# A four-layer diffusion trunk on one core: the time mixing of the even layers gathers its output channel-major, with the states as stationary operands and centred values

## The chip, the cores and the metric

The kernel runs on one core of a Trainium2 chip. The metric is the device time of one execution in microseconds (us). Engines are named as the profile does: PE is TensorE (PEld its weight loads), DVE is VectorE, ACT is ScalarE, POOL is GpSimd, SP is SyncE, which here issues DMAs.

## The reference

The reference is a trunk of four layers over 256 latent and 256 context tokens, 1024 channels, float32. Every layer has a mixer and a channel mixer, with modulation vectors from a conditioning input. In layers 0 and 2 the mixer is time mixing (RWKV-7, both directions, 8 heads of 64 channels) beside neighbourhood attention; in layers 1 and 3 it is another pair, which the change does not touch. Per head the time mixing is

```python
def step(s, inp):
    r_t, w_t, k_t, v_t, a_t, b_t = inp
    sa = jnp.einsum('bhvk,bhk->bhv', s, a_t)
    s = s * w_t[:, :, None, :] + sa[..., None] * b_t[:, :, None, :] + v_t[..., None] * k_t[:, :, None, :]
    return s, jnp.einsum('bhvk,bhk->bhv', s, r_t)
...
def readout(y, r, v, dirs, g):
    mean = jnp.mean(y, axis=-1, keepdims=True)
    var = jnp.mean(jnp.square(y - mean), axis=-1, keepdims=True)
    y = (y - mean) * lax.rsqrt(var + A_GN_EPS) * ln_g.reshape(A_HEADS, A_HEAD_DIM) + ln_b.reshape(A_HEADS, A_HEAD_DIM)
    bonus = sum(jnp.sum(r * kt * r_k, axis=-1, keepdims=True) for _, kt, _ in dirs) * v
    return ((y + bonus).reshape(g.shape) * g).astype(g.dtype)
```

The two directions' outputs are added before the readout. The state is linear in the values, row by row: each value channel has a row of the state and a channel of the output of its own. So an output less its mean over a head's channels is the output that values less their mean over these channels give.

## The kernel before

The 512 tokens stand side by side as eight chunks of 64. A unit of the time mixing is one pair of heads and one direction: 4 x 2 = 8 units in an even layer, 16 in the kernel. `pre` (L580, once per pair) reads the shifted projections, normalises the keys (key norms L598, their reciprocal root on POOL L600, the copy L567 that spreads it over channels) and transposes the values to token-major through PSUM (`transp`, L571 to L577, a copy on ACT). `front` (L610, per unit) makes decays and scaled rows, the products inside a chunk (L674, and the value product L704) and the start of a triangular inverse; `mid` (L708) merges the inverse (L888 and others) and makes for each chunk a matrix Phi that takes the state before it to the state after it, a matrix RW that takes the state to the output, G (masked products of rows inside a chunk), UV (both sources of the state) and B (what the chunk adds).

`rec` (L758) is the recurrence. It first writes the in-chunk product of all eight chunks into one PSUM bank pO (L769, 32 passes), and then walks the chunks. At each of seven steps it multiplies RW with the state and adds that into pO (the output product, L790); at six of them it also makes the next state (the state product, two passes at L784, then the decay and the addition of B on DVE, L793). Before, pO is token-major: 128 tokens by two heads of 64 channels. So that one pass serves both heads, ACT copies the two halves of a state to the diagonal blocks of a zeroed 128 x 128 tile (L789, two copies a step, four such tiles in turn):

```python
for h in range(2):
    hs = slice(64 * h, 64 * h + 64)
    nc.scalar.copy(wide[hs, hs], st[hs])
nc.tensor.matmul(pO[cs, t, :], RW[:, t, c2, :], wide, start=False, stop=d == 1, skip_group_check=True)
```

`readout` (L796, once per pair, behind its second direction) reduces pO to a mean (L802, L803), subtracts it (L806), squares (ACT, L807), reduces (L809), scales and adds the constant (L810), takes the reciprocal root on POOL (L812), scales by it (L813) and multiplies values and bonus (L816), all per token on DVE where nothing else is said. Its second half, `late` (L822), transposes result and bonus to channel-major on PE, applies the layer's scale and shift, adds, multiplies with the gate and stores.

What sets the order: the class `Pipe` (L1819) hands over, for each i, `front` of unit i, `mid` of unit i-1 in step with `rec` of unit i-2, then the `late` of the pair before, then a `readout`, all at a high priority; the large weight products of the layer (`gemm`, weights cast on ACT L190 and split on DVE L191, three passes L222 to L224) and the modulation vectors of the next layer (`mod_units`, weights mw by DMA, product L165) fill the rest. A tile scheduler takes this program, with dependences and priorities, and sets each engine's order; an engine then works its list strictly in that order.

Of the kernel before, what the change touches and what calls it, by code (L numbers as in the profile page):

```python
# [20 lines left out]
F32 = mybir.dt.float32  # L21
# [9 lines left out]
NT = 512  # L31
# [11 lines left out]
class Mixed:  # L43
    """Outputs of the mixers, channel-major, kept in DRAM by channel tile."""
# [12 lines left out]
class Net:  # L57
    def __init__(self, tc, a, ctx):
# [6 lines left out]
        # banks of PSUM by use: large products, parts of the mixers, adaLN, outputs of the mixers  # L65
# [14 lines left out]
    def load_consts(self, name, pool, tag=None, width=None):  # L80
        """A table of constants that depend on shapes alone; its parts become attributes."""
        nc = self.nc
        off, n = CONST_OFF[name]
        t = pool.tile([128, width or n], F32, name=tag or "cst_" + name)[:, :n]
        nc.sync.dma_start(t, self.a["k_" + name])
        for part, (o, w) in off.items():
            setattr(self, part, t[:, o:o + w])
# [55 lines left out]
    def mod_units(self, l, pool=None):  # L143
        """Six chunks of eight channel tiles for each stream, channel-major: [128, 48, 2].

        The weights of the first two chunks come through the pool, if one is given."""
# [9 lines left out]
        for u in range(0, 48, 8):  # L156
            if u == 16:
                pool = None
            # two units on each quarter of the partitions
# [20 lines left out]
    def unit(self, src, kt, cols):  # L180
        """src [128, kt, cols] in DRAM -> high and low tiles."""
# [12 lines left out]
    def mm3(self, out, pairs, start=True, stop=True):  # L194
        """out += sum over (lhsH, lhsL, rhsH, rhsL) of lhs.T @ rhs."""
# [7 lines left out]
    def gemm(self, W, kt, c0, cols, xh, xl, tok, done, order=None):  # L203
        """Columns c0.. of W (given as [128, kt, n]), channel-major: done(column tile, psum) for each 128."""
# [23 lines left out]
    def gemm_tok(self, W, c0, cols, xh, xl, done):  # L228
        """Columns of W, token-major: done(token tile, first column, width, psum)."""
# [21 lines left out]
    def vecs(self, pool, name, **src):  # L251
        """Vectors of multiples of 128 in DRAM, channel-major [128, n] each; they become attributes of the result."""
# [20 lines left out]
    def square_sums(self, tok):  # L273
        """Sums of h^2 over the channels, token-major: [128, token tile]."""
# [13 lines left out]
    def rstd_bcast(self, tok, ss=None):  # L288
        """1 / sqrt(mean of h^2 + eps) on all partitions: [128, tokens]."""
# [16 lines left out]
    def norm_mod(self, l, g, which, tok, ss=None):  # L306
        """nH, nL: high and low parts of the modulated RMSNorm, channel-major."""
# [124 lines left out]
def rows(x):  # L432
    """The four rows of the grid in a padded line of tokens."""
    return x[:, 1:261].rearrange("p (r w) -> p r w", w=65)[:, :, :64]


def rwkv_consts():
# [4 lines left out]
    # for a and for r, by the chunk of a tile: the mask of b on the chunk's half of the partitions, that of k on the other  # L442
# [14 lines left out]
class Rwkv:  # L457
    """Both directions of the time mixing for one layer, by pairs of heads."""
# [3 lines left out]
    def __init__(self, net, e, pool):  # L462
# [18 lines left out]
        self.sts = [pool.tile([128, 128], F32, name=f"st{i}") for i in range(4)]  # L481
        self.nst = 0
        # a of one unit, and r of three
        self.ar = pool.tile([128, 4, NT], F32, name="ar")
        self.nar = 0
        for b in [self.shb] + self.sts:
            nc.gpsimd.memset(b, 0.0)
        self.pd = {}

# [1 line left out]
    def project(self, key, i, col, nh, nl):  # L491
        """Column tile col of the input projection as tile i of a group."""
# [13 lines left out]
    def shifted(self, key, cols):  # L506
        """A group of projections, mixed with the shift of the tokens."""
# [14 lines left out]
        for i, c in enumerate(cols):  # L522
# [7 lines left out]
            else:  # L530
                # the two chunks of each tile in each other's place
# [18 lines left out]
    def tok_sums(self, prod, out):  # L550
        """out [128 tokens, tile, head] = sums over the channels of each head."""
# [4 lines left out]
    def tok_sums_swapped(self, prod, out):  # L556
        """The same, with the two chunks of each tile in each other's place."""
# [6 lines left out]
    def bcast_heads(self, small, out):  # L564
        """out [channels of two heads, tokens] from small [tokens, tile, head]."""
# [6 lines left out]
    def transp(self, src, dst):  # L572
        """dst [128, 4, 128] token-major from src [128, 512] channel-major."""
# [6 lines left out]
    def pre(self, hp):  # L580
# [9 lines left out]
        # normalised keys  # L590
# [11 lines left out]
        # token-major values, each chunk on the half of the partitions that its own rows do not use  # L602
        S["V"] = pl.tile([128, 4, 128], F32, name="V", bufs=2)
        self.transp(v, S["V"])
# [4 lines left out]
    def front(self, hp, d, S):  # L609
# [30 lines left out]
        # scaled rows: a and b (both time reversed inside chunks for d = 1), r, k  # L640
# [3 lines left out]
        # those of a chunk side by side, b first in even chunks and k in odd ones  # L644
# [16 lines left out]
        # products with a inside each chunk of a tile: those of b on the chunk's half of the partitions, those of k on the other  # L661
        Q = [n.tmp.tile([128, 4, 2, 64], F32, name=name) for name in ("nt", "sq")]
        # [rows of b and k, products with r] by chunk and head
# [18 lines left out]
        # bonus: r * k * r_k, summed over the channels of a head and over the directions  # L682
# [7 lines left out]
        # token-major copies  # L690
# [1361 lines left out]
```

## Time and profile before

| | |
|---|---|
| time, median of 3 runs (lowest to highest) | 3420.98 us (3409.43 to 3421.87) |
| span of the profiled execution | 3398.9 us |
| own time of the profiled execution | not given apart from the three runs, which are 10.5 to 23 us longer than the span |
| instructions in the profile | 63286 |
| PE / PEld busy | 92% / 71% |
| DVE / ACT / POOL busy | 56% / 38% / 15% |
| moved by DMA | 479.21 MB, mean 141 GB/s |

The profile is of one execution, by the hardware profiler. Its page gives busy time by engine; other views give the same for a stretch of time, the waits (which engine stood idle before which line, and what ended the idle time), and the instructions in order of time. A row of a wait reads "engine, tile and line that waited <- engine, tile and line (or DMA) that ended the wait". In rows of PE the start times of neighbours tell what a pass costs, since passes overlap at their ends; "64\*64" is the form of the stationary operand. A granted clock of 1.00 is TensorE's level of 2.4 GHz, and 0.50 that of 1.2 GHz.

### The profile page before, as it was taken

The page shows a single profiled execution, that of the slowest core. Times are in us where ns is not written, and L with a number is a line of the kernel's source. Part 1 is how long each engine was busy: PE and PEld are TensorE (multiplying, and loading weights), DVE is VectorE, ACT ScalarE, POOL GpSimd, SP SyncE. Part 2 cuts the span into 40 slices and gives each one's busy share as a digit, 9 for nine tenths or more (in the row PEclk, how much of TensorE's full clock was granted, in tenths as well). Part 3 has the DMA queues.
Part 4 walks back from the last instruction along what each step waited for, and adds up shares of the span by engine and source line. Part 5 has one row for each costly group of instructions (what it writes and reads, how often), then busy time and mean ns, then how long its engine had stood idle before and what let it go on. Part 6 is the DMA issues. An engine that isn't in the chain of part 4 may idle for free. (4 is left out here: it accounts for less than half of the span.)

```text
span 3398.9 us, 63286 instructions
## 1 busy us (share of the span) xinstructions
PE 3120.2 (92%) x24452; PEld 2418.1 (71%) x24452; DVE 1920.1 (56%) x4229; ACT 1291.6 (38%) x2785; POOL 515.4 (15%) x1159
## 2 busy tenths in 40 slices
PE   7999789999999889899999998877999999977998
PEld 4876456787787667578887776545787777756997
DVE  3556545766436696343434556555676445685554
ACT  3334344332235335232223333434333224534444
POOL 0223310000001653000000123220000000563000
PEclk8998889999999899899998998889999999978999
DMA  8635655345345544733336634553334334644554
GB/s 282 178 97 130 151 141 156 87 136 143 111 125 143 167 126 144 245 119 94 96 100 191 184 103 128 126 125 101 102 127 136 111 113 145 196 156 156 160 176 134
DMA packets 549696, 479.21 MB, mean 141 GB/s; under 512 B 176533, under 2 KB 480531, under 8 KB 549395
## 3 DMA queue, kind: packets, MB, share of 16 engines
q1 hardware_dynamic: 549394, 475.17, 48.5%
q8 instruction: 193, 3.16, 0.4%
q14 instruction: 109, 0.89, 0.1%
HBM read 406.34 MB, written 72.90 MB: 141 GB/s over the span
## 5 line engine op out<-in xcount | busy, mean ns | idle before, releaser
L191 DVE TENSOR_TENSOR wl<-w,wh 128x512 fp32r<-128x512 f32 x786 | 545.8, 697 | 766.4 <-ACT wh L190 746.6
L190 ACT CAST wh<-w 128x512 fp32r<-128x512 f32 x786 | 484.5, 619 | 1159.7 <-PE pb L223 343.3
L222 PE MATMUL pg<-nh,wh 128*128 128x512 f32 (+2 forms) x760 | 294.6, 388 | 19.4 <-ACT nh L270 8.7
L222 PE MATMUL pb<-nh,wh 128*128 128x512 f32 (+1 forms) x832 | 305.3, 374 | 4.0 <-ACT nh L325 2.7
L223 PE MATMUL pb<-nl,wh 128*128 128x512 f32 (+1 forms) x832 | 306.5, 371 | 0.0
L224 PE MATMUL pb<-nh,wl 128*128 128x512 f32 (+1 forms) x832 | 299.8, 373 | 0.0
L223 PE MATMUL pg<-nl,wh 128*128 128x512 f32 (+2 forms) x760 | 291.4, 383 | 0.6 <-DVE gr L1179 0.6
L224 PE MATMUL pg<-nh,wl 128*128 128x512 f32 (+2 forms) x760 | 290.4, 382 | 0.1
L298 POOL TENSOR_TENSOR nr<-nv,cst_base 128x4 f32<-128x4 f32 (+1 forms) x9 | 8.4, 938 | 1660.8 <-DVE nv L296 1660.8
L222 PE MATMUL ph<-nh,wh 128*128 128x512 f32 (+1 forms) x624 | 242.0, 388 | 10.1 <-ACT nh L325 5.9
L224 PE MATMUL ph<-nh,wl 128*128 128x512 f32 (+1 forms) x624 | 240.1, 385 | 0.0
L223 PE MATMUL ph<-nl,wh 128*128 128x512 f32 (+1 forms) x624 | 239.5, 384 | 0.0
L165 PE MATMUL px<-mw,cnd 128*32 128x256 f32 x1536 | 158.8, 450 | 83.5 <-DMA mw<-in_mod_w_dram 68.9
L222 PEld LDWEIGHTS pg<-nh,wh 128*128 128x128 f32 (+1 forms) x760 | 146.3, 193 | 56.4 <-ACT nh L270 11.3
L222 PEld LDWEIGHTS pb<-nh,wh 128*128 128x128 f32 x832 | 158.6, 192 | 36.3 <-ACT nh L325 3.2
L223 PEld LDWEIGHTS pb<-nl,wh 128*128 128x128 f32 x832 | 159.5, 192 | 29.3 <-DVE nl L271 1.3
L224 PEld LDWEIGHTS pb<-nh,wl 128*128 128x128 f32 x832 | 155.5, 191 | 30.7 <-issue 1.0
L223 PEld LDWEIGHTS pg<-nl,wh 128*128 128x128 f32 (+1 forms) x760 | 146.1, 192 | 34.8 <-issue 3.0
L224 PEld LDWEIGHTS pg<-nh,wl 128*128 128x128 f32 (+1 forms) x760 | 145.7, 192 | 29.1 <-issue 1.0
L858 POOL TENSOR_TENSOR Etmp<-E 64x14 f32<-64x14 f32 (+13 forms) x448 | 160.6, 359 | 31.1
L860 POOL TENSOR_TENSOR E<-E,Etmp 64x14 f32<-64x14 f32 (+13 forms) x448 | 158.8, 354 | 32.9
L222 PEld LDWEIGHTS ph<-nh,wh 128*128 128x128 f32 x624 | 119.6, 192 | 39.7 <-ACT nh L325 6.7
(578 smaller groups left out, 6440.8 us busy)
## 6 DMA issues: line engine op xcount, KB each, us to landing
mw<-in_mod_w_dram SPq DMA_DIRECT2D x192, 512.0 KB
w<-in_f_gate_dram SPq DMA_DIRECT2D x176, 256.0 KB
w<-in_f_up_dram SPq DMA_DIRECT2D x176, 256.0 KB
w<-in_f_down_dram SPq DMA_DIRECT2D x176, 256.0 KB
w<-in_w_in_even_dram SPq DMA_DIRECT2D x104, 256.0 KB
w<-in_w_in_odd_dram SPq DMA_DIRECT2D x80, 256.0 KB
w<-in_w_out_dram SPq DMA_DIRECT2D x64, 256.0 KB
hd<-hT SPq DMA_DIRECT2D x32, 256.0 KB
```

The source lines that it names most:

```text
L165: nc.tensor.matmul(p[32 * c:32 * c + 32, :256], self.cnd[:, k, :], wt[:, 256 * c:256 * c + 256], start=k == 0, stop=k == KT - 1, skip_grou ...
L190: nc.scalar.copy(wh[:, :n], w[:, :n])
L191: nc.vector.tensor_tensor(wl[:, :n], w[:, :n], wh[:, :n].bitcast(F32), op=ALU.subtract)
L222: nc.tensor.matmul(o, wh[:, kk, m:m + mm], xh[:, k, tok], start=i == 0, stop=False)
L223: nc.tensor.matmul(o, wh[:, kk, m:m + mm], xl[:, k, tok], start=False, stop=False)
L224: nc.tensor.matmul(o, wl[:, kk, m:m + mm], xh[:, k, tok], start=False, stop=i == kt - 1)
L298: nc.gpsimd.tensor_tensor(r, v, self.mhalf[:, :nt], op=ALU.pow)
L858: nc.gpsimd.tensor_tensor(o, E[:, :s, s:s + 1].to_broadcast([m8, s, v]), E[:, s:s + 1, s + 1:].to_broadcast([m8, s, v]), op=ALU.mult)
L860: nc.gpsimd.tensor_tensor(E[:, :s, s + 1:], E[:, :s, s + 1:], o, op=ALU.add)
```

## The change

The output bank pO becomes channel-major: two heads of 64 channels on the partitions, eight chunks of 64 tokens. For the in-chunk product the operands trade places (UV stationary, G moving), and a pass writes the partition half of its head instead of its chunk's. The output product becomes two passes of 64 x 64 per step, with the state as stationary operand and RW moving; the copies to the wide tiles and these tiles are gone, with their eight zero fills on POOL. Since a mean over a head's channels would now run over partitions, `pre` subtracts from the values their mean over each head, and keeps that mean. `readout` copies pO to SBUF (ACT), squares it (ACT), sums the squares per token with `tok_sums` (PE, eight passes into a bank of PSUM), and takes scale and root as before; values and bonus are multiplied after the mean was added back, by halves of the partitions. `late` spreads the reciprocal root over channels (`bcast_heads`: a copy on DVE, four transposes on PE) and multiplies with it on DVE, before layer scale and shift; the transposes of the result are gone. Line numbers move by some lines, since comments are left out in the changed file. The diff, without that:

```diff
 class Rwkv.__init__
-        self.sts = [pool.tile([128, 128], F32, name=f"st{i}") for i in range(4)]
-        self.nst = 0
-        for b in [self.shb] + self.sts:
-            nc.gpsimd.memset(b, 0.0)
+        nc.gpsimd.memset(self.shb, 0.0)
 pre
-        self.transp(v, S["V"])
+        pv = n.bank("f")
+        for t in range(4):
+            nc.tensor.transpose(pv[:, t * 128:(t + 1) * 128], v[:, t * 128:(t + 1) * 128], n.ident)
+        pv = pv.rearrange("p (a c) -> p a c", c=64)
+        S["mean"] = mean = pl.tile([128, 8], F32, name="mean", bufs=4)
+        nc.vector.tensor_reduce(mean, pv, axis=AX.X, op=ALU.add)
+        nc.vector.tensor_scalar(mean, mean, 1.0 / 64, None, op0=ALU.mult)
+        nc.vector.tensor_tensor(S["V"].rearrange("p t (h c) -> p (t h) c", h=2), pv,
+                                mean[:, :, None].to_broadcast([128, 8, 64]), op=ALU.subtract)
 rec
-            S["pO"] = n.bank("o", (128, 4, 128))
+            S["pO"] = n.bank("o", (128, 8, 64))
...
-                    nc.tensor.matmul(pO[64 * c2:64 * c2 + 64, t, hs], G[:, 1, 2 * t + c2, h, :], UV[:, t, c2, hs],
-                                     start=d == 0 and t == 0 and h == 0, stop=False, skip_group_check=True)
+                    nc.tensor.matmul(pO[hs, 2 * t + c2, :], UV[:, t, c2, hs], G[:, 1, 2 * t + c2, h, :],
+                                     start=d == 0 and t == 0 and c2 == 0, stop=False, skip_group_check=True)
...
-            wide = self.sts[self.nst % 4]
-            self.nst += 1
             for h in range(2):
                 hs = slice(64 * h, 64 * h + 64)
-                nc.scalar.copy(wide[hs, hs], st[hs])
-            nc.tensor.matmul(pO[cs, t, :], RW[:, t, c2, :], wide, start=False, stop=d == 1, skip_group_check=True)
+                nc.tensor.matmul(pO[hs, c, :], st[hs], RW[hs, t, c2, :], start=False, stop=d == 1, skip_group_check=True)
 readout
-        mean = n.tmp.tile([128, 8], F32, name="mean")
-        nc.vector.tensor_reduce(mean, o, axis=AX.X, op=ALU.add)
-        nc.vector.tensor_scalar(mean, mean, 1.0 / 64, None, op0=ALU.mult)
         y, sq = yt.tile(), yt.tile()
-        c = y.rearrange("p (a v) -> p a v", v=64)
-        nc.vector.tensor_tensor(c, o, b8(mean), op=ALU.subtract)
-        nc.scalar.activation(sq, y, AF.Square)
+        nc.scalar.copy(y, pO)
+        s2 = n.tmp.tile([128, NT], F32, name="sq")
+        nc.scalar.activation(s2, y, AF.Square)
+        ps = n.bank("b")
+        self.tok_sums(s2, ps)
         var = n.tmp.tile([128, 8], F32, name="var")
-        nc.vector.tensor_reduce(var, sq.rearrange("p (a v) -> p a v", v=64), axis=AX.X, op=ALU.add)
-        nc.vector.tensor_scalar(var, var, 1.0 / 64, 64e-5, op0=ALU.mult, op1=ALU.add)
+        nc.vector.tensor_scalar(var, ps[:, :8], 1.0 / 64, 64e-5, op0=ALU.mult, op1=ALU.add)
...
-        nc.vector.tensor_tensor(c, c, b8(rs), op=ALU.mult)
...
-            nc.vector.tensor_tensor(sq[p].rearrange("p (t h v) -> p t h v", t=4, h=2),
-                                    S["d"][1]["UV"][p, :, c2].rearrange("p t (h v) -> p t h v", h=2),
-                                    S["bonus"][p].rearrange("p (t h) -> p t h", h=2)[:, :, :, None].to_broadcast([64, 4, 2, 64]),
-                                    op=ALU.mult)
+            z = sq[p].rearrange("p (a v) -> p a v", v=64)
+            u = z.rearrange("p (t h) v -> p t h v", h=2)
+            nc.vector.tensor_tensor(u, S["d"][1]["UV"][p, :, c2].rearrange("p t (h v) -> p t h v", h=2),
+                                    S["mean"][p].rearrange("p (t h) -> p t h", h=2)[:, :, :, None].to_broadcast([64, 4, 2, 64]),
+                                    op=ALU.add)
+            nc.vector.tensor_tensor(z, z, b8(S["bonus"], p), op=ALU.mult)
 late
-            pt = n.bank("b")
-            for t in range(4):
-                nc.tensor.transpose(pt[:, t * 128:(t + 1) * 128], y[:, t * 128:(t + 1) * 128], n.ident)
-            nc.scalar.activation(y, pt, AF.Identity, scale=self.lg[:, hp:hp + 1], bias=self.lb[:, hp:hp + 1])
+            pr = n.bank("b")
+            self.bcast_heads(rs, pr)
+            nc.vector.tensor_tensor(y, y, pr, op=ALU.mult)
+            nc.scalar.activation(y, y, AF.Identity, scale=self.lg[:, hp:hp + 1], bias=self.lb[:, hp:hp + 1])
```

Since a scheduler sets the order, three places of it follow, before and after. On PE, the first two steps of the first recurrence (pb is a PSUM bank of parts of the mixer, po the output bank, st a state, Bst the first one, L888 the inverse and L674 the chunk products of other units); before:

```order
L784 MATMUL pb<-Bst,Phi 64x64 [waits DVE_49]
L784 MATMUL pb<-Bst,Phi 64x64
L790 MATMUL po<-st_426,RW 64x128 [waits Activation_49]
L888 MATMUL pb<-Yb,Rinv 16x16 x24
L674 MATMUL pf<-ar,bk 128x128 [waits DVE_49]
L674 MATMUL pf<-ar,bk 128x128 [waits PE_49]
L674 MATMUL pf<-ar,bk 128x128 x6
L888 MATMUL pb<-Yb,Rinv 16x16 x7
L784 MATMUL pb<-st,Phi 64x64 [waits DVE_49]
L784 MATMUL pb<-st,Phi 64x64
L790 MATMUL po<-st_427,RW 64x128 [waits Activation_49]
```

and the same place in the changed kernel, where the state product is L790, the output product L793, and the other units' lines are L889 and L680:

```order
L790 MATMUL pb<-Bst,Phi 64x64 [waits DVE_49]
L790 MATMUL pb<-Bst,Phi 64x64
L793 MATMUL po<-RW,Bst 64x64 x2
L889 MATMUL pb<-Yb,Rinv 16x16 [waits Activation_49]
L889 MATMUL pb<-Yb,Rinv 16x16 x20
L680 MATMUL pf<-ar,bk 128x128 [waits DVE_49]
L680 MATMUL pf<-ar,bk 128x128 [waits PE_49]
L680 MATMUL pf<-ar,bk 128x128 x6
L889 MATMUL pb<-Yb,Rinv 16x16 x11
L790 MATMUL pb<-st,Phi 64x64 [waits DVE_49]
L790 MATMUL pb<-st,Phi 64x64
L793 MATMUL po<-RW,st 64x64 x2
```

The output product stands behind the state product in both; what moved is that it no longer waits for ACT and comes as two passes.

On DVE, `pre` of the first pair of heads (kn are the key norms, kr POOL's reciprocal root, wl a weight's low part, lw a decay); before:

```order
L598 TENSOR_SCALAR kn<-pf 128x8 [waits PE_49]
L567 COPY nt<-kr 128x512 [waits Pool_49]
L191 TENSOR_TENSOR wl<-w,wh 128x512 [waits DVE_49,DMAHW4_49,PE_49,Activation_49]
L191 TENSOR_TENSOR wl<-w,wh 128x512 [waits DMAHW7_49,PE_49,Activation_49]
L621 TENSOR_SCALAR lw<-lw 128x512 [waits Activation_49]
```

and now:

```order
L595 TENSOR_SCALAR kn<-pf 128x8 [waits PE_49]
L607 TENSOR_REDUCE mean<-pf 128x8 [waits PE_49]
L608 TENSOR_SCALAR mean<-mean 128x8 [waits DVE_49]
L609 TENSOR_TENSOR V<-pf,mean 128x512 [waits DVE_49]
L564 COPY nt<-kr 128x512 [waits Pool_49]
L191 TENSOR_TENSOR wl<-w,wh 128x512 [waits DMAHW4_49,PE_49,Activation_49]
L191 TENSOR_TENSOR wl<-w,wh 128x512 [waits DMAHW7_49,PE_49,Activation_49]
L627 TENSOR_SCALAR lw<-lw 128x512 [waits Activation_49]
```

The three instructions on the values came in between the key norms and the copy that waits for POOL.

On ACT, around the second readout (yo is a tile of outputs, naqk and naqh are queries and keys of the attention, naP its weights); before:

```order
L732 COPY UV<-pb 64x2x128 x2
L1016 ACTIVATE naP,sm<-pg,mx 128x256 [waits DVE_49]
L1024 COPY naPT<-ph 128x4x128 [waits PE_49]
L807 ACTIVATE yo<-yo 128x512 [waits DMAHW6_49,DVE_49]
L620 ACTIVATE lw<-pf,w0h 128x512 [waits PE_49]
```

and now:

```order
L738 COPY UV<-pb 64x2x128 x2
L803 COPY yo<-po 128x512 [waits PE_49]
L998 CAST naqk<-naqk 64x512 [waits DMAHW3_49]
L805 ACTIVATE sq<-yo 128x512 [waits Activation_49]
L270 CAST naqh<-naqk 128x512 [waits DMAHW4_49]
L997 CAST nakh<-naqk 64x512
```

The square before waited for DVE's subtraction; now it follows ACT's own copy of the bank, with a cast that waits for a DMA between the two.

## Rows read from the trace of the kernel before

**Rows 1.** The page: busy time by engine, and TensorE's granted clock in 40 equal slices (tenths).

```profile
PE 3120.2 (92%) x24452; PEld 2418.1 (71%) x24452; DVE 1920.1 (56%) x4229; ACT 1291.6 (38%) x2785; POOL 515.4 (15%) x1159
...
PEclk8998889999999899899998998889999999978999
```

**Rows 2.** Stretches from:to in us; length, busy per engine, clock, DMA share, GB/s.

```profile
100.00:290.00 190.00, 183.72 (x1981) 144.84 (x1979) 107.49 (x249) 72.85 (x164) 47.81 (x135) 0.97 0.47 126
290.00:560.00 270.00, 221.35 (x2944) 139.80 (x2943) 153.98 (x385) 118.00 (x313) 62.52 (x139) 0.82 0.58 142
```

**Rows 3.** Waits of PE, 100 to 2400 us: total us, times, longest.

```profile
PE px L165 <- DMA mw<-in_mod_w_dram: 50.9, 33, 6.3
...
PE pb L784 <- DVE st L793: 6.9, 5, 3.6
```

**Rows 4.** Same stretches as rows 2, L790 alone: PE, PEld, clock, DMA, GB/s.

```profile
100.00:290.00 190.00, 5.88 (x26) 2.58 (x26) 0.97 0.47 126
```

**Rows 5.** PE in order of time: start us, duration us, instruction.

```profile
212.97 0.33 PE L784 MATMUL pb<-st,Phi 64*64 64x64 f32 x4
213.23 0.43 PE L790 MATMUL po<-st,RW 128*64 128x128 f32 x2
213.59 0.50 PE L222 MATMUL pg<-nh,wh 128*128 128x512 f32 x1
```

**Rows 6.** Two short stretches, columns as in rows 2; the clock is third from last.

```profile
212.00:214.00 2.00, 2.00 (x48) 1.56 (x45) 1.56 (x7) 0.73 (x2) 0.00 (x0) 1.00 0.31 91
...
347.00:350.00 3.00, 3.00 (x40) 2.08 (x40) 0.70 (x3) 0.78 (x2) 1.65 (x8) 0.50 0.93 256
```

**Rows 7.** PE in order of time: the value product (L704), first pair and what follows.

```profile
135.24 0.27 PE L704 MATMUL pf<-V,nt 64*64 64x64 f32 x1
135.25 0.27 PE L704 MATMUL pf<-V,sq 64*64 64x64 f32 x1
...
136.32 0.69 PE L618 MATMUL pf<-tw,lora 64*128 64x512 f32 x1
```

**Rows 8.** PE in order of time: the same product, later in the mixer.

```profile
347.80 0.37 PE L704 MATMUL pf<-V,nt 64*64 64x64 f32 x1
...
349.71 0.37 PE L769 MATMUL po<-UV,bkg 128*64 128x64 f32 x2
```

**Rows 9.** PE in order of time: the in-chunk product (L769) and what follows.

```profile
409.32 1.15 PE L769 MATMUL po<-UV,bkg 128*64 128x64 f32 x32
410.40 0.33 PE L1021 MATMUL ph<-cst_base,naP 128*128 128x128 f32 x1
```

**Rows 10.** PE in order of time: sums over a head's channels (L553).

```profile
98.63 0.95 PE L553 MATMUL pf<-cst_rwkv,sq 128*128 128x2 f32 x8
```

**Rows 11.** Groups by line, shapes apart: busy, mean ns; idle before, releasers.

```profile
L789 ACT COPY st<-st 64x64 f32<-64x64 f32 x192 | 46.4, 242 | 78.6 <-DVE st L793 74.0 <-DVE sm L1017 1.5
...
L790 PE MATMUL po<-st,RW 128*64 128x128 f32 x224 | 52.5, 323 | 2.0 <-ACT st L789 1.9
...
L790 PEld LDWEIGHTS po<-st,RW 128*64 128x64 f32 x224 | 22.9, 146 | 21.6 <-issue 7.6 <-ACT st L789 4.6 <-ACT naP L1016 1.5
```

**Rows 12.** The line's instructions: ns min/median/max, first and last start, forms.

```profile
L802 DVE TENSOR_REDUCE mean<-po x8: 678/688/692, 292.3 to 2347.6; 128x8 f32<-128x512 f32 x8
...
L816 DVE TENSOR_TENSOR yo<-UV,bonus x16: 674/686/689, 301.6 to 2351.8; 64x512 f32<-64x512 f32 x16
```

**Rows 13.** DVE in order of time, at two places: idle before and releaser last.

```profile
190.01 0.43 DVE L567 COPY nt<-kr 128x512 f32<-128x512 f32 x1 [1.76 <-POOL kr L600]
...
416.93 0.69 DVE L813 TENSOR_TENSOR yo<-yo,rsn 128x512 f32<-128x512 f32 x1 [3.47 <-POOL rsn L812]
```

**Rows 14.** Waits of DVE, 100 to 2400 us.

```profile
DVE yo L813 <- POOL rsn L812: 20.7, 6, 7.9
...
DVE nt L567 <- POOL kr L600: 18.2, 7, 4.9
```

**Rows 15.** Waits of ACT, 100 to 2400 us.

```profile
ACT naqk L997 <- DMA naqk<-qkd: 58.6, 13, 9.7
```

More of the change, by code (lines that the diff above doesn't have):

```diff
@@ L774, in rec @@
             t, c2 = c // 2, c % 2
-            cs = slice(64 * c2, 64 * c2 + 64)
             if j == 0:
@@ L797, in readout @@
         nc, n, pl = self.nc, self.n, self.p
-        pO = S["pO"]
-        o = pO.rearrange("p t (h v) -> p (t h) v", h=2)
-        b8 = lambda x: x[:, :, None].to_broadcast([128, 8, 64])
-        mean = n.tmp.tile([128, 8], F32, name="mean")
-        nc.vector.tensor_reduce(mean, o, axis=AX.X, op=ALU.add)
-        nc.vector.tensor_scalar(mean, mean, 1.0 / 64, None, op0=ALU.mult)
-        y, sq = yt.tile(), yt.tile()
-        c = y.rearrange("p (a v) -> p a v", v=64)
-        nc.vector.tensor_tensor(c, o, b8(mean), op=ALU.subtract)
@@ L807, in readout @@
-        nc.scalar.activation(sq, y, AF.Square)
+        pO = S["pO"].rearrange("p c s -> p (c s)")
+        y, sq = yt.tile(), yt.tile()
+        nc.scalar.copy(y, pO)
[3 more added lines that the diff above has]
+        self.tok_sums(s2, ps)
         var = n.tmp.tile([128, 8], F32, name="var")
-        nc.vector.tensor_reduce(var, sq.rearrange("p (a v) -> p a v", v=64), axis=AX.X, op=ALU.add)
-        nc.vector.tensor_scalar(var, var, 1.0 / 64, 64e-5, op0=ALU.mult, op1=ALU.add)
+        nc.vector.tensor_scalar(var, ps[:, :8], 1.0 / 64, 64e-5, op0=ALU.mult, op1=ALU.add)
@@ L811, in readout @@
         rs = n.tmp.tile([128, 8], F32, name="rsn")
         nc.gpsimd.tensor_tensor(rs, var, n.mhalf, op=ALU.pow)
-        nc.vector.tensor_tensor(c, c, b8(rs), op=ALU.mult)
+        b8 = lambda x, p: x[p][:, :, None].to_broadcast([64, 8, 64])
         for c2 in range(2):
             p = slice(64 - 64 * c2, 128 - 64 * c2)
-            nc.vector.tensor_tensor(sq[p].rearrange("p (t h v) -> p t h v", t=4, h=2),
-                                    S["d"][1]["UV"][p, :, c2].rearrange("p t (h v) -> p t h v", h=2),
-                                    S["bonus"][p].rearrange("p (t h) -> p t h", h=2)[:, :, :, None].to_broadcast([64, 4, 2, 64]),
-                                    op=ALU.mult)
+            z = sq[p].rearrange("p (a v) -> p a v", v=64)
[4 more added lines that the diff above has]
+            nc.vector.tensor_tensor(z, z, b8(S["bonus"], p), op=ALU.mult)
```

## The prediction

> **What bounds the kernel now.** I read the page first. TensorE is busy for 3120.2 of 3398.9 us, and its granted clock dips in the slices where the mixers of layers 0 and 2 lie [rows 1]. The stage windows come next, because shares over the whole span hide this: the change touches only the two even mixers, about 100 to 560 us and 1895 to 2360 us. Each has two parts; the rows are layer 0's, and layer 2 repeats them within 2%. In the first 190 us TensorE is busy for 183.72 us at clock 0.97: a microsecond of TensorE is a microsecond of time. In the rest it is busy for 221.35 of 270 us at clock 0.82, so it waits for 49 us there, about 100 in the two layers [rows 2]. Who ends the waits, from layer 0 to layer 2, is the third view. The weights of the modulation vectors (mw) end 50.9 us; what this change touches ends little directly, 6.9 us by the state on VectorE [rows 3]. The fourth view is where the output product stands: 26 of the 112 passes of a layer, 23%, lie in the saturated part [rows 4].
>
> **The change, part by part.** The working runs over 16 recurrences (8 per layer), each with seven output products, six of them next to a state product.
>
> *Output product.* At the upper clock (1.00) a step's state product takes 212.97 to 213.23 = 0.26 us and the wide output product 213.23 to 213.59 = 0.36 us [rows 5, 6]. The order shows the new product directly behind the state product, in its 64-by-64 form. What four such passes cost when they follow others of the form: 32 passes of the value product take 1.08 us at the upper clock (135.24 to 136.32) [rows 7]; taking the first four as a state product, 28 are left in 0.82 us, 0.12 us for four. So a step goes from 0.62 to 0.38 us, and the lone seventh product from 0.36 to the state product's 0.26. A recurrence saves 6 x 0.24 + 0.10 = 1.5 us. At the lower clock (0.50) the same 32 passes take 347.80 to 349.71 = 1.91 us [rows 6, 8], 1.77 times as long, so there it is 2.7 us. The clock of 0.97 and 0.82 in the stretches means the lower level for 6% and 36% of the time [rows 2]; with 23% and 77% of the products there, 29%. Sixteen times 0.71 x 1.5 + 0.29 x 2.7 is **30 us** off TensorE (24 to 43 with either clock alone).
>
> *In-chunk product.* Its 32 passes take 1.08 us (409.32 to 410.40) with the two column halves taking turns [rows 9]. The swapped operands write columns in the order low, low, high, high, so fewer neighbours can overlap. No row shows that order. If all overlap stays, it costs nothing. If none does, each pass takes what a pair takes in [rows 7], 0.82 / 14 = 0.058 us: 32 x 0.058 = 1.9 us, 0.8 more, 13 us over 16. Half of the neighbours still differ, so I take **+7**.
>
> *Token sums.* The variance moves from VectorE to TensorE: eight passes take 0.95 us to the end of the last [rows 10], some 0.1 of it beside the next block; eight times, **+7 us**. The transposes of values, scales and bonus are as many as before.
>
> TensorE: -30 + 7 + 7 = -16 us. The 23% in the saturated parts count whole (-3.7 us). Of the rest I take half (-6.2 us), because the modulation weights already end half of the waits there and a faster TensorE meets them sooner. **About -10 us.**
>
> *ScalarE* loses 224 copies of 0.242 us (54 us), each of which held back its queue: 74.0 us of idle time before them end with the state [rows 11]. Only 1.9 us of TensorE's idle time, or 6.5 with its weight loads, ends at them [rows 11]. Between 0 and -6.5 I take **-2**, near the row of the matmuls. The copy of the values goes, and a copy of the output, of the same shape, comes.
>
> *VectorE, values less their mean.* Reduction, scale and subtraction are priced by the same steps of today's readout: 0.69 us for the reduction [rows 12], 0.69 for an elementwise pass of the size, L813 [rows 13], and little for the scale of eight columns, together 1.5 us, eight times. The order puts them between the key norms and the copy that waits for POOL; VectorE sits idle there 18.2 us in seven times, 2.6 us each [rows 14], and at 190.01 such a wait is 1.76 us long [rows 13]. So 0; without that cover +12.
>
> *VectorE, readout.* Mean, subtraction and reduction of the squares go (three passes of 0.69); two additions over half the partitions (0.69 each) and a broadcast copy (0.43) come, 1.8 us [rows 12, 13]. The scaling only moves. More important is the wait that goes from its queue: 20.7 us in six times for POOL's reciprocal root [rows 14]; at 416.93 the scaling, and what is queued behind it, waits 3.47 us [rows 13]. The consumer of that root now runs a unit later, except for the last pair of heads. VectorE is busy for 57% of the late part (153.98 of 270) [rows 2], so a wait there often delays nothing. I take a good third, **-8**, and **+3** for the token sums on which the variance now waits; the bounds are -21 and 0.
>
> Eight memsets less on POOL and no DMA more or less: 0, POOL is busy for 15% [rows 1].
>
> Sum: -10 - 2 - 8 + 3 = **-17 us**. The profiled span would go from 3398.9 to 3382 us; the shown runs are 10.5 to 23 us longer than the span, and which of them was profiled is not given, so I set the sum against the median: 3421 - 17 = **3404 us**. The order of the odd mixers shifts too, though nothing in them is edited; the two even mixers, ordered differently, take 460 and 465 us today, so I expect a few microseconds from that, of either sign.
>
> **The rivals.**
> 1. *More comes through.* The TensorE saving whole (-16), the weight loads' 6.5, three quarters of VectorE's 20.7 (-15) and no new wait: -37, **3384 us**. For it: three queues lose waits in one chain. Against it: rows 3 name other work for most of TensorE's idle time.
> 2. *Hidden anyway.* In the late parts TensorE only reaches the modulation weights sooner, and no neighbours overlap in the in-chunk product (+13 instead of +7): the saturated parts give 0.23 x 10 = -2 us, VectorE and ScalarE nothing, **3418 us**. For it: 50.9 us of mw waits.
> 3. *Slower: the token sums stop TensorE.* They wait for a copy and a square on ScalarE; in the order a cast that waits for a DMA stands between these two, and such casts wait up to 9.7 us, 58.6 us in 13 times [rows 15]. TensorE takes its work in order, so the rest of the mixer would stand behind. Of the 17 us nothing is left from 2.1 us on average over eight readouts; at 5 us it is 40 - 17, **3444 us**. Against it: the scheduler puts in-chunk and weight products before them.
> 4. *Two row halves in one bank.* The value product's passes start 0.01 us apart in pairs, and its pairs come from both row halves and go to one PSUM tile [rows 7]; I count the new product as such pairs. The rival is that its two heads take turns instead: 0.12 us more for each of 112 products, 13 us, of which (as above) 0.6 count, +8: **3412 us**. The Trainium skill, TensorEngine Tiling (Array Packing), section Restrictions and Gotchas, has the rule for this: different row tiles cannot use the same PSUM bank at once. By it the sum would be -9; the trace speaks against it for this form, since the pairs start together.
>
> **How the numbers follow.** Forecast 0.45 (its own spread 3395 to 3413), rival 1 0.17, rival 2 0.19, rival 3 0.14, rival 4 0.05. A measurement of this kernel can tell about 0.5%, 17 us, from no change. The forecast lies on that bound: half of it counts as faster, and with rival 1 and a little of the others for the shifted order that is 0.41. Same: the other half, rivals 2 and 4, a part of 3: 0.46. Slower: 0.13. The range, 3384 to 3430, reaches down to rival 1 and up over rivals 2 and 4 and the low end of rival 3.
>
> **What would show it.** Right: the new output product's passes follow the state product's by some 0.03 us each, and the pair's block takes about 0.4 us at the upper clock; no ScalarE copies of the state; the idle time before the readout's scaling gone, VectorE's wait before the key-scale copy shorter; TensorE's idle time in the late parts about as long as now. The in-chunk product's 32 passes tell their term: 1.1 us or 1.9. Wrong: token sums with TensorE idle before them (rival 3), mw waits well over 51 us with the mixers as long as now (rival 2), heads of the output product 0.06 us apart instead of together (rival 4). It would also be wrong if the time moved in the odd layers or the channel mixers instead.

## The result, and the profile after

The changed kernel takes 3468.5 us (median of 4 runs, 3461.06 to 3477.39) where the kernel before takes 3421.43: ratio 1.0141, 95% interval 1.0111 to 1.0170. It is slower by some 48 us, and outside the range that was forecast. The profiled execution has a span of 3471.0 us. The page, with the lines that answer to [rows 1]:

```profile
span 3471.0 us, 63614 instructions
...
PE 3123.7 (90%) x24740; PEld 2425.4 (70%) x24740; DVE 1926.6 (56%) x4245; ACT 1243.7 (36%) x2561; POOL 518.5 (15%) x1151
...
PEclk9988788999999798999999998777999999977999
```

TensorE is busy as long as before, ScalarE 48 us less: what was added is idle time. The two stretches of [rows 2]:

```profile
100.00:290.00 190.00, 182.77 (x2008) 146.16 (x2008) 102.94 (x235) 62.98 (x130) 49.40 (x136) 0.94 0.48 129
290.00:560.00 270.00, 213.29 (x3000) 137.89 (x2998) 149.92 (x390) 95.04 (x219) 61.27 (x137) 0.81 0.56 136
```

and L793, the new output product, alone in them, as [rows 4]:

```profile
100.00:290.00 190.00, 5.04 (x56) 3.78 (x56) 0.94 0.48 129
290.00:560.00 270.00, 15.05 (x160) 10.96 (x160) 0.81 0.56 136
```

In the second stretch TensorE is busy 8 us less and idle 8 us more; the output product takes 15.05 us there and 5.04 in the first (5.88 before). The new step itself is as it was priced. A state product (L790) with its output product (L793) at clock 1.00, and the in-chunk product (L776) with its new order of columns; PE in order of time, as [rows 5] and [rows 9]:

```profile
204.35 0.33 PE L790 MATMUL pb<-st,Phi 64*64 64x64 f32 x4
204.51 0.28 PE L793 MATMUL po<-RW,st 64*64 64x64 f32 x4
204.72 0.50 PE L223 MATMUL pg<-nl,wh 128*128 128x512 f32 x1
...
510.41 1.20 PE L776 MATMUL po<-bkg,UV 128*64 128x64 f32 x32
511.54 0.33 PE L1022 MATMUL pg<-cst_base,naP 128*128 128x128 f32 x1
```

The step takes 204.35 to 204.72 = 0.37 us (0.38 was forecast, 0.62 before), the in-chunk product 1.13 us (1.08 before). The waits of PE from 100 to 2400 us, as [rows 3]:

```profile
PE px L165 <- DMA mw<-in_mod_w_dram: 84.9, 33, 13.5
PE po L793 <- DVE Bst L761: 15.9, 1, 15.9
PE pb L883 <- DVE Bst L761: 12.1, 1, 12.1
...
PE pb L790 <- DVE st L796: 4.9, 5, 3.6
```

The modulation weights end 34 us more than before, and two single waits for Bst (what a chunk adds to the state) 28 us. No row names the token sums (L550) as what TensorE waited in.

Where the time went by stage is read from the weight products, of which all kernels have as many: the start of the n-th pass of L222. The profiled execution of before (span 3398.9) lies below the bulk of its runs, so the column to compare with is e9, an edit of before with the same order and the same time (below; span 3406.6). Columns other than e9's are differences from it, in us; the column of before, -1.3 to -9.7, tells how far two executions of one order lie apart.

| pass of L222, what it follows | e9, us | before | after | e3 | e15 | e14 | e5 |
|---|---|---|---|---|---|---|---|
| 177th, mixer of layer 0 | 560.3 | -1.3 | +14.1 | +19.7 | +3.1 | -5.5 | +8.5 |
| 1013th, mixer of layer 1 | 1440.7 | -9.7 | +25.2 | +28.9 | +16.1 | -3.9 | +9.1 |
| 1585th, within the channel mixer of layer 1 | 1882.9 | -9.4 | +32.8 | +34.1 | +14.3 | -5.4 | +15.3 |
| 1746th, mixer of layer 2 | 2390.9 | -7.0 | +46.2 | +57.6 | +16.9 | -5.1 | +15.8 |
| 2509th, mixer of layer 3 | 3154.3 | -5.6 | +67.5 | +71.5 | +25.2 | +0.5 | +23.3 |

The changed kernel's span is 64 us longer than e9's. On this scale 14 and 13 of these come in the two even mixers; the other 37 come where nothing was edited.

### The profile page after: what moved, and what is told of

Same layout as the page of the kernel before. It is cut to its first block, busy times and chain, and to the rows that moved or that the text cites. A ratio compares the mean times of both kernels' runs of the same rounds, so it can differ in the third digit from the quotient of the medians.

```text
span 3471.0 us, 63614 instructions
## 1 busy us (share of the span) xinstructions
PE 3123.7 (90%) x24740; PEld 2425.4 (70%) x24740; DVE 1926.6 (56%) x4245; ACT 1243.7 (36%) x2561; POOL 518.5 (15%) x1151
## 5 line engine op out<-in xcount | busy, mean ns | idle before, releaser
L222 PE MATMUL pb<-nh,wh 128*128 128x512 f32 (+1 forms) x832 | 305.6, 375 | 11.0 <-ACT wh L190 3.2
L222 PE MATMUL pg<-nh,wh 128*128 128x512 f32 (+2 forms) x760 | 296.3, 390 | 15.7 <-ACT nh L270 9.9
L222 PE MATMUL ph<-nh,wh 128*128 128x512 f32 (+1 forms) x624 | 241.6, 387 | 9.8 <-ACT nh L325 5.8
L222 PEld LDWEIGHTS pb<-nh,wh 128*128 128x128 f32 x832 | 158.7, 192 | 43.6 <-ACT wh L190 5.1
L222 PEld LDWEIGHTS pg<-nh,wh 128*128 128x128 f32 (+1 forms) x760 | 147.3, 194 | 55.0 <-issue 11.6
L861 POOL TENSOR_TENSOR E<-E,Etmp 64x14 f32<-64x14 f32 (+13 forms) x448 | 169.9, 379 | 33.0
L165 PEld LDWEIGHTS px<-mw,cnd 128*32 128x32 f32 x1536 | 40.8, 119 | 172.1 <-DMA mw<-in_mod_w_dram 117.0
```

What stands on the lines that cost most here:

```text
L165: nc.tensor.matmul(p[32 * c:32 * c + 32, :256], self.cnd[:, k, :], wt[:, 256 * c:256 * c + 256], start=k == 0, stop=k == KT - 1, skip_grou ...
L222: nc.tensor.matmul(o, wh[:, kk, m:m + mm], xh[:, k, tok], start=i == 0, stop=False)
L861: nc.gpsimd.tensor_tensor(E[:, :s, s + 1:], E[:, :s, s + 1:], o, op=ALU.add)
```

## The experiments

Three theories were set up. A: the readout's squares and the spread reciprocal root take buffers of shared rings, so that the next pair's front can't run ahead any more. B: the new chain of copy, squares and token sums stops TensorE. C: any edit makes the scheduler draw a new order, and that order is worse. To tell them apart some kernels keep an order: behind the program stands

```diff
+    for d in steps.split():
+        at += int(d)
+        if last is not None:
+            tc.add_manual_dep(own[at], last.name, info, reason="pin")
+        last = own[at]
```

where `own` are an engine's instructions, `steps` a table with the order wanted, and `info` an edge that fixes the order of issue alone. "The order of before" means this for the instructions that both kernels have (27,003 of some 27,700 in the whole change); new ones find their own place. Ratios are to the kernel before, with 95% intervals.

### The order by itself

**e3**, the kernel before, in the order of after:

> The kernel before, unedited, with every instruction that both kernels have kept in the order in which it stands in the changed kernel. Theories A and C: the loss comes without the change, 3470 to 3490 us (the 48 us, and the 10 to 20 us of work that it saves are not saved here), of which about 33 us in the two odd layers. Theory B: 3415 to 3430 us.

1.0149 (1.0125 to 1.0173), 3466.57 us, 46 us above before and 3 us under what was expected by A and C: with none of the change's work, the whole loss. B falls as its main cause.

**e7** and **e8**, small edits of before elsewhere, in the scheduler's own order:

```diff
-            nc.gpsimd.memset(b, 0.0)
+            nc.vector.memset(b, 0.0)
...
-        nc.vector.tensor_copy(X["D"], eGc[:, :, 63 if d == 0 else 0])
+        nc.gpsimd.tensor_copy(X["D"], eGc[:, :, 63 if d == 0 else 0])
```

> The kernel before, with the zero fills of the five scratch tiles at the start of each even layer on VectorE instead of POOL: ten instructions in the whole kernel, nothing near the recurrence. In the scheduler's order 635 of VectorE's 4229 instructions and 2009 of TensorE's 17654 move against each other. Theory C: 3440 to 3475 us, as far from before as the changed kernel. Theory A: 3415 to 3430 us.

> The kernel before, with one copy of 128 x 8 per unit (the chunk decays, 16 in the kernel, 0.15 us each) on POOL instead of VectorE; 701 of VectorE's instructions move in the scheduler's order. Theory C: 3430 to 3475 us. Theory A: 3415 to 3430 us.

e7 is at 1.0101 (1.0070 to 1.0133), e8 at 1.0172 (1.0150 to 1.0195), 3476 us, a microsecond above what C allows: C. **e9** is e8's edit in the order of before:

> The edit of e8 (a copy of 128 x 8 per unit on POOL), with all other instructions of each engine in the order of the kernel before. If e8's 58 us are the order alone: 3410 to 3425 us, no difference from before that can be measured. If the copy on POOL or the listing of the order itself costs: above 3435 us.

0.9994 (0.9980 to 1.0009). The 58 us of e8 are the order, and holding an order costs nothing that can be told. **e15** puts only what lies outside the even mixers in the order of after:

> The kernel before, unedited: instructions of the two even mixers in the order of before among themselves, all others (odd layers, channel mixers, projections) in the order of the changed kernel. If the loss is spread over the program as the stages of the changed kernel's trace say, half or more of the 46 us comes from here: 3438 to 3450 us. If it lies in the even mixers: 3415 to 3425 us.

1.0057 (1.0037 to 1.0077): some 20 of the 46 us come from parts that the change doesn't touch, a little under the half that was expected. In the table 13 of them come in the mixer of layer 1 and 8 between the mixers of layers 2 and 3. The other 26 are left for the order within the even mixers; no run has that alone.

### The shared buffers

**e4** is the kernel before with one buffer taken from a ring, **e1** and **e6** the changed kernel with its buffers taken out of the rings:

```diff
 e4, before
-        nc.scalar.activation(sq, y, AF.Square)
+        s2 = n.tmp.tile([128, NT], F32, name="sq")
+        nc.scalar.activation(s2, y, AF.Square)
...
 e1, changed kernel
-        s2 = n.tmp.tile([128, NT], F32, name="sq")
+        s2 = pl.tile([128, NT], F32, name="s2")
...
-        b = self.n.tmp.tile([128, 8, 64], F32, name="nt")
+        b = self.n.tmp.tile([128, 8, 64], F32, name="nt") if own is None else own.tile([128, 8, 64], F32, name="rsb")
...
 e6, e1 and
-        ps = n.bank("b")
+        ps = S["pO"].rearrange("p c s -> p (c s)")
```

> The kernel before, with one edit: the squares of its readout go to a buffer of the shared ring sq instead of the tile that later holds the bonus. No instruction more or less. Theory A, if the one ring is enough: 3440 to 3470 us. Theory B: 3415 to 3430 us. Theory C: anywhere between 3400 and 3480 us.

> The changed kernel, with the squares of the readout and the spread reciprocal roots each in a tile of their own instead of a buffer of the shared rings sq and nt (two buffers each, handed out in the order of the program). Theory A (the rings: the next pair's front, which takes buffers of the same rings later in the program, can no longer run ahead of a readout, and the scheduler's order follows from that): most of the loss goes, 3400 to 3430 us. Theory B (the token sums and the copies before them stop TensorE in themselves): 3455 to 3475 us, as the changed kernel. Theory C (the scheduler's order changes at random with any edit): anywhere between 3390 and 3480 us, and the odd layers' part moves as well.

> The same three buffers moved, but the scheduler's own order again. Theory A (what the shared buffers tie is the loss, and without it the scheduler does as well as before): 3410 to 3430 us. Theory C (a new order is a new draw): 3430 to 3470 us, near e1, though it has the same work as e5.

e4 is at 1.0158 (1.0138 to 1.0179), 3471 us, a microsecond above what A allows and well within C; e1 at 1.0103 (1.0076 to 1.0130) and e6 at 1.0113 (1.0090 to 1.0136), which A doesn't: without the rings most of the loss stays. A new order without a shared buffer (e8) is as bad as one with it (e4). The rings matter in another way: with the squares and the spread root in them, the order of before isn't possible at all, since there the next pair takes its buffers of sq and nt ahead of the readout (in the trace of before its products write sq from 285 us on, the first readout's square starts at 300 us), while by the program the readout's turn in the ring comes first. That is why e2 and its followers have e1's tiles.

The six kernels in an order of their own lie at 1.0141, 1.0103 and 1.0113 with the change's work, and at 1.0158, 1.0101 and 1.0172 with that of before: the spread hides any difference between the two. All six lie above before and none below, so the order of before is a good one among those that the scheduler gives; why, no run shows.

### One pair of the order

In the changed kernel VectorE and TensorE at the longest of the two waits for Bst, in order of time:

```profile
349.35 0.43 DVE L878 STREAM_TRANSPOSE Xinv<-Yb 32x256 f32<-32x256 f32 x1 [14.10 <-DMA Yb<-scr]
...
352.88 0.68 DVE L761 TENSOR_TENSOR Bst<-pb,Dk 128x512 f32<-128x512 f32 x1
...
353.62 0.48 PE L793 MATMUL po<-RW,Bst 64*64 64x64 f32 x4 [15.87 <-DVE Bst L761]
```

Bst needs nothing from the inverse, but stands behind its transposes in VectorE's queue. **e13** turns this pair round, at both places:

> The changed kernel with its own order kept instruction by instruction, except that at two places of VectorE's order the step that makes what a chunk adds to the state (Bst, L761) stands before the transposes of the inverse (L878) instead of behind them. There the transposes waited 14.1 and 10.4 us for a transfer, and TensorE 15.9 and 12.1 us for Bst. If single pairs of this kind carry the loss: 28 us less, 3440 us. If what is behind is bound by the inverse anyway, or the loss is spread: 3458 to 3470 us.

1.0112 (1.0084 to 1.0141), 9 us less than the changed kernel where 28 had to come if single pairs carried the loss, and a difference within the noise of the two. In e13, VectorE in order of time:

```profile
337.61 0.69 DVE L761 TENSOR_TENSOR Bst<-pb,Dk 128x512 f32<-128x512 f32 x1 [0.34 <-PE pb L759]
351.24 0.43 DVE L878 STREAM_TRANSPOSE Xinv<-Yb 32x256 f32<-32x256 f32 x1 [12.94 <-DMA Yb<-scr]
```

and the waits of PE from 100 to 2400 us:

```profile
PE px L165 <- DMA mw<-in_mod_w_dram: 72.8, 32, 13.4
PE pb L833 <- DVE yo L825: 16.4, 2, 16.0
PE pb L883 <- DVE Xinv L878: 14.2, 10, 10.1
```

Bst is there 15 us earlier, the transposes wait as before, and TensorE's 15.9 us come back at the next step behind them (L833, 16.0). These waits for Bst were the place where the lateness showed; taking them away did not bring their time back.

### The parts, in the order of before

**e10** has the centred values alone, **e11** the new recurrence alone, **e14** both (z is half of the tile that the readout adds, w spreads a number per token and head over the head's channels):

```diff
 e10, before with pre as in the change, and in the readout
+            nc.vector.tensor_tensor(z, S["d"][1]["UV"][p, :, c2].rearrange("p t (h v) -> p t h v", h=2), w(S["mean"]), op=ALU.add)
+            nc.vector.tensor_tensor(z, z, w(S["bonus"]), op=ALU.mult)
...
 e11, before with rec as in the change, and in the readout
-        o = pO.rearrange("p t (h v) -> p (t h) v", h=2)
+        o = pO
```

> The kernel before with the centred values alone: the mean over a head taken from the values in pre, and added back in the readout before the bonus; recurrence and readout otherwise as before, order of before for all kept instructions. The forecast priced the three passes in pre at 0, covered by the wait for POOL (3416 to 3424 us here, with 8 x 1.4 us of additions on VectorE hidden too). If they lie on the path that sets the end: 8 x 1.5 + 8 x 1.4 = 23 us, 3430 to 3442 us.

> The kernel before with the new recurrence alone: in-chunk product with its operands in each other's place, output products with the state as stationary operand, no copies on ScalarE; the readout's instructions are those of before, on a bank that is now channel-major, so that mean, variance and scale are taken over tokens and the output isn't the reference's. Order of before for all kept instructions. In the other runs the state and output products cost 20 us less of TensorE in all, the in-chunk product the same. If 0.6 of that counts, and 2 us of ScalarE, as the forecast has it: 3402 to 3410 us. If it is hidden (the modulation weights are waited for instead): 3415 to 3422 us. If the 14 us that e2 and e5 lost lie in the recurrence: 3425 to 3435 us.

> Centred values and the new recurrence together, readout as in e10 on a bank that is now channel-major (mean, variance and scale are taken over tokens, so that the output isn't the reference's); order of before for all kept instructions. If the loss of e2 and e5 lies in the readout: 3410 to 3422 us, the sum of e10 and e11. If the two parts together lose it: 3428 to 3436 us.

e10 is at 1.0012 (0.9998 to 1.0027), e11 at 0.9992 (0.9977 to 1.0007), e14 at 0.9982 (0.9964 to 1.0000). The centred values cost nothing that can be told. The recurrence gains 0.08% alone (-0.07 to 0.23%) and, from e10 to e14, 0.30% (0.07 to 0.53%), 3 and 10 us, with TensorE's products 20 us cheaper over the kernel. The stretch from 290 to 565 us, e9, e11 and e14:

```profile
290.00:565.00 275.00, 232.65 (x2969) 148.76 (x2965) 155.46 (x390) 118.79 (x315) 63.79 (x142) 0.80 0.59 144
```

```profile
290.00:565.00 275.00, 212.97 (x3016) 139.39 (x3013) 154.69 (x390) 99.13 (x231) 63.62 (x139) 0.84 0.59 144
```

```profile
290.00:565.00 275.00, 225.38 (x3015) 148.87 (x3015) 162.92 (x400) 99.24 (x231) 64.52 (x139) 0.80 0.58 143
```

and the longest row of the waits of PE from 100 to 570 us, e9, e11 and e14:

```profile
PE px L165 <- DMA mw<-in_mod_w_dram: 18.8, 12, 3.5
```

```profile
PE px L165 <- DMA mw<-in_mod_w_dram: 28.4, 13, 6.3
```

```profile
PE px L165 <- DMA mw<-in_mod_w_dram: 19.5, 11, 3.3
```

In e11 TensorE is busy 20 us less in this stretch than in e9, but only some 9 of the 20 are in the edited products (from each pass's start to the next, idle time left out); the rest is in lines that both kernels have alike, at a granted clock of 0.84 instead of 0.80. In e14, at 0.80, TensorE is busy 7 us less. The mixer ends 1.8 us sooner in e11 and 5.5 in e14 (177th pass). That the rest of the saving turns into waits for the modulation weights isn't shown: they are 10 us longer in e11, but not in e14, and before itself, of e9's order and time, has 26.1 us of them. What these runs show is that, where TensorE is idle for 40 to 60 of 275 us, less work of its own comes through only in part.

**e2** is the whole change with own tiles, **e5** the same with the sums in the output bank (e6's work):

> The same kernel as e1, with every instruction that both kernels have kept, engine by engine, in the order in which it stands in the kernel before; only the new instructions find their own place. Theories A and C (the loss is in the order, the saved work is real): 3395 to 3410 us, 10 to 25 below the kernel before, and the odd layers take as long as in it. Theory B: 3440 us or more, with TensorE idle before the token sums or what follows them.

> As e2 (own tiles, kept instructions in the order of before), but the token sums go into the output bank itself, which has just been copied out, instead of a third user of the two banks b. In e2 two merges of other units wait 8.5 and 3.1 us for the step that reads the sums (pb L883 <- DVE var L809), and the sums wait 5.5 us for the squares. If these waits cost what they show: 12 us under e2, 3418 to 3426 us. If they stood beside other waits: 3430 to 3437 us, and the other 14 us over the kernel before lie in work that was priced too low.

e2 is at 1.0060 (1.0036 to 1.0083), e5 at 1.0046 (1.0025 to 1.0066). The bank isn't it. Against e14 the readout costs 0.6%, some 20 us. By the table (e5 less e14) 14 of them come in the mixer of layer 0 and 8 in the channel mixer of layer 1, where nothing was edited; the mixer of layer 2, which has as many readouts, takes 0.2 us more. So it doesn't look like a price per readout, and in the order of after it can't be seen at all: there the kernel with the change's work (1.0141) is no slower than the one without (e3, 1.0149). Three attempts to find it followed. **e12** moves the sums into `late`; **e16** moves, in e5's order, the copy that spreads the root some 15 us back on VectorE, **e17** the first token sums too:

> As e2 (own tiles, order of before), but token sums, variance and reciprocal root stand in the second half of the readout, one unit later, where nothing is behind them that the next unit waits for. In e2 TensorE waited 5.5 us for the squares and 11.6 us for the bank. If these waits were its loss: 3415 to 3424 us. If not: 3428 to 3438 us as e2 and e5.

> The kernel of e5 with its order kept instruction by instruction, except that on VectorE the copy that spreads the reciprocal root (L564) stands some 15 us further back in the six readouts that have time for it (TensorE takes it 40 to 50 us later; the last pair of each layer is left). If VectorE's waits for POOL there (25.0 us in e5) carry the readout's cost: 3410 to 3422 us. If VectorE has slack and they cost nothing: 3426 to 3437 us, as e5.

> e16, and the first four token sums of the first readout of layer 0 stand 43 instructions further back on TensorE, right ahead of the next in-chunk product, where the squares are there (4.5 us of waiting in e5). If that wait counts: 2 to 5 us under e16. If not: as e16, within 3 us.

e12 is at 1.0102 (1.0078 to 1.0127), no better than e2 and rather worse. e16 is at 1.0032 (1.0016 to 1.0048), e17 at 1.0053 (1.0033 to 1.0073). The waits of VectorE from 100 to 2420 us, first e5, then e16:

```profile
DVE rsb L564 <- POOL rsn L811: 25.0, 5, 7.8
```

```profile
DVE rsb L564 <- POOL rsn L811: 1.8, 1, 1.8
```

23 us of waiting left VectorE's queue, and the time moved by 0.14% (between 0.40% less and 0.12% more), some 5 us at best guess; e17, which has the same move, is back at e5's ratio. The waits don't cost what they show. In these two traces the readout's cost shows in TensorE's wait for the modulation weights in the late units of layer 0; the waits of PE from 410 to 572 us, e14 and then e5:

```profile
PE px L165 <- DMA mw<-in_mod_w_dram: 6.3, 5, 2.0
```

```profile
PE px L165 <- DMA mw<-in_mod_w_dram: 19.9, 9, 5.2
```

The same wait is 10.9 us in before, 6.6 in e9 and 13.2 in e17, which is as slow as e5, so this is a hint and no proof. What the readout's cost is in the order of before stays open.

## Why the prediction was wrong

- **The step that failed** is the sentence on the order: the odd mixers' order shifts, and "I expect a few microseconds from that, of either sign". In its place the runs show +46 us by the order alone (e3), some 20 of them outside the even mixers (e15); the order within the even mixers, to which the other 26 are left, had no term at all. Its ground was bad: the two even mixers, though ordered differently, both belong to one order, that of before, and so say nothing on a new one. e7 and e8 show what an order drawn anew takes: 1 to 1.7% more. That cost is no part of the change's work, and no row of the trace of before could have priced it; but the range could have allowed for it. The forecast's last sign of being wrong came true: 37 of the 64 us in the table come in the odd layers and the channel mixers.
- **Output product, -30 us of TensorE.** The step's 0.37 us is right; from every pass's start to the next, idle time left out, state and output products take 71.3 us before and 51.3 after, 20 us less. The side of the change was priced right (some 50 us by the forecast's prices), that of before too high (some 80). With the next two terms TensorE's work went down by 12 us where 16 were forecast, because the errors partly cancel; that is luck.
- **In-chunk product, +7.** 23.2 us before, 23.1 after: no cost; the overlap doesn't need the halves to take turns column by column.
- **Token sums, +7.** Right: 7.7 us for the new sums.
- **Half of TensorE's late saving counts; ScalarE -2.** By the forecast's prices (-30 and +7, of which 0.6 count, and -2) some 16 us were to come from the recurrence. In the order of before it gains 3 us alone (e11) and 10 us on top of the centred values (e14 against e10); the two intervals meet between 2 and 8 us. So less came through than was forecast, and what held the rest back isn't shown.
- **Centred values, 0.** Right (e10), and by the reason given: VectorE's wait before the key-scale copy is 3.4 us in after and 5.7 in e5, against 18.2 [rows 14].
- **Readout, -8 + 3.** Wrong in two places. The reader of the root was said to run a unit later; in the changed kernel its copy does run 27 to 38 us behind the start of the root, and without a wait, in four of eight readouts, but 1.7 us behind it in the other four, and of the wait that was to go (20.7 us, [rows 14]) 11.4 us are there. In e5's order the copy runs 2 to 9 us behind in all eight, and the wait is 25.0 us. And e16 took 23 us of it away without a gain that can be told, so that -8 had little ground either way. In the order of before the readout costs some 20 us.
- **Rivals.** 3 named the right sign and a time 24 us too low, with a wrong mechanism: TensorE doesn't wait in the token sums in after, and 4.5 us once in e5. 4 fell: the four passes of the output product shown above start at 204.512, 204.518, 204.570 and 204.577 us, so the two heads of a pair start 0.007 us apart, and 0.007 is the median over the 58 groups of four at the upper clock that run without idle time; by the rival it would be 0.06. The Trainium skill, TensorEngine Tiling (Array Packing), section Restrictions and Gotchas, says that different row tiles cannot access one PSUM bank at the same time. As far as starts tell, the trace stands against this for passes of this form, as [rows 7] did.

## What to carry to other kernels

Where a scheduler works out the order from the whole program, an edit is measured together with a new draw of the order: here edits with next to no work of their own cost 1 to 1.7%, as much as the change. Compare a change in a held order, or several draws of both, before its work is blamed; and look which buffers of a shared ring it takes, because they can make the old order impossible. In a part where the busiest engine already waits a fifth of the time, price low what you take off it until the chain of waits says otherwise, and test a long wait by moving it: one of the longest here came back at the next step, another left without a gain that could be told. And before a stretch of two traces is compared, look what two executions of one kernel differ by in it.

## What was not expected of the hardware

TensorE's passes of the in-chunk product (128 rows, 64 columns of the stationary operand) overlap as well when half of the neighbours write the same column half (1.13 us for 32 passes) as when they take turns (1.08 us). In a stretch of 275 us TensorE was granted 0.80 in e9 and e14, 0.82 in before and e5 and 0.84 in e11, and half of the 20 us that it was busy less in e11 than in e9 are in lines that both have alike: its busy time in a stretch tells the clock as well as the work. And executions of one kernel differ by 1%: the 12 runs of e5 lie between 3415 and 3448 us, so that a trace of one execution doesn't tell half a per cent.
